# A row sum on one core: 127 consecutive rows to a partition, the last 128 rows one to a partition, and two stores on two queues

## The chip, the cores and the metric

The kernel runs on one core of a Trainium2 chip. The time is the device time of one execution in microseconds (us).

A profile names engines: DVE is VectorE, ACT is ScalarE, SP is SyncE. "SPq" and "ACTq" are the sequencers of SP and ACT issuing DMAs. HBM is the chip's main memory, where the input and the output lie; a partition is one of the 128 rows of the on-chip memory. A DMA is a copy between the two: the DMA engines carry it out in packets, and each engine that takes part reports a completion. "Landing" is the moment at which a DMA's completion has fully arrived.

## The reference

```python
batch, seq, dim = 32, 512, 1024
x = np.random.randn(batch, seq, dim).astype(np.float32)     # 67.1 MB
def reference(x, multiplier):                                # multiplier 0.5
    return (np.sum(x, axis=-1) * multiplier).astype(np.float32)
```

Seen flat, 16,384 rows of 4 KiB each become 16,384 floats (64 KiB).

## The kernel before

Each of the 128 partitions owns 128 consecutive rows. Seven blocks of 16 rows a partition (8.39 MB each) stream through three buffers; DVE reduces half of a block in one instruction, ACT the other half row by row. The eighth block comes in pieces of 8, 5 and 2 rows and one row cut in two, so that little work is left when the last byte arrives. Then one store writes everything.

```python
    rows = N // P                                            # 128
    x_rows = x_flat.rearrange("(p c) d -> p c d", p=P)       # partitions 512 KiB apart
    out_view = out.rearrange("b s -> (b s)").rearrange("(p c) -> p c", p=P)
    # ... seven blocks: nc.sync.dma_start(out=t, in_=x_rows[:, c0 : c0 + B, :])
    pieces = [(0, 8), (8, 13), (13, 15)]
    # ... the pieces, then the last row in two: in_=x_rows[:, c0 + B - 1, lo:hi]
    dve_span(t, B - 1, 0, cut, part)                         # first 640 columns of the last row
    dve_span(t, B - 1, cut, D, res[:, rows - 1 : rows], start=part)
    # ... a wait of the sync queue for the loads and ACT
    store = nc.sync.dma_start(out=out_view, in_=res)         # 128 runs of 512 bytes
```

Of the kernel before, what the change touches and what calls it, by code (L numbers as in the profile page):

```python
# [1 line left out]

# [4 lines left out]


@with_exitstack
def kernel(  # L10
    ctx: ExitStack,
    tc: tile.TileContext,
    x: bass.AP,
    multiplier: float,
    out: bass.AP,
):







    nc = tc.nc
    P = nc.NUM_PARTITIONS
    fp32 = mybir.dt.float32
    ADD = mybir.AluOpType.add

    x_flat = x.flatten_outer_dims()
    N, D = x_flat.shape  # L30
    rows = N // P
    x_rows = x_flat.rearrange("(p c) d -> p c d", p=P)
    out_view = out.rearrange("b s -> (b s)").rearrange("(p c) -> p c", p=P)
    mul = float(multiplier)

    B = 16
    n_blocks = rows // B
    assert N == P * rows and rows == n_blocks * B

    x_pool = ctx.enter_context(tc.tile_pool(name="x", bufs=3))  # L40
    res_pool = ctx.enter_context(tc.tile_pool(name="res", bufs=1))
    sums = res_pool.tile([P, rows], fp32, name="sums")
    res = res_pool.tile([P, rows], fp32, name="res")
    part = res_pool.tile([P, 1], fp32, name="part")

    loads = []
    acts = []

    def act_row(t, r, col):
        acts.append(nc.scalar.activation(  # L50
            out=t[:, r, :],
            in_=t[:, r, :],
            func=mybir.ActivationFunctionType.Copy,
            scale=mul,
            accum_out=res[:, col : col + 1],
        ))

    def dve_span(t, r, lo, hi, dst, start=0.0):
        mid = (lo + hi) // 2
        nc.vector.tensor_tensor_reduce(  # L60
            out=t[:, r, lo:mid],
            in0=t[:, r, lo:mid],
            in1=t[:, r, mid:hi],
            scale=mul,
            scalar=start,
            op0=ADD,
            op1=ADD,
            accum_out=dst,
        )

    for b in range(n_blocks - 1):
        c0 = b * B
        t = x_pool.tile([P, B, D], fp32, name="xb")
        loads.append(nc.sync.dma_start(out=t, in_=x_rows[:, c0 : c0 + B, :]))  # L74
        h = B // 2
        nc.vector.reduce_sum(  # L76
            out=sums[:, c0 : c0 + h], in_=t[:, 0:h, :], axis=mybir.AxisListType.X
        )
        nc.vector.tensor_single_scalar(  # L79
            out=res[:, c0 : c0 + h],  # L80
            in_=sums[:, c0 : c0 + h],
            scalar=mul,
            op=mybir.AluOpType.mult,
        )
        for r in range(h, B):
            act_row(t, r, c0 + r)

    c0 = (n_blocks - 1) * B
    t = x_pool.tile([P, B, D], fp32, name="xb")
    cut = 640  # L90
    pieces = [(0, 8), (8, 13), (13, 15)]
    for lo, hi in pieces:
        loads.append(
            nc.sync.dma_start(  # L94
                out=t[:, lo:hi, :], in_=x_rows[:, c0 + lo : c0 + hi, :]
            )
        )
    for lo, hi in ((0, cut), (cut, D)):
        loads.append(
            nc.sync.dma_start(  # L100
                out=t[:, B - 1, lo:hi], in_=x_rows[:, c0 + B - 1, lo:hi]
            )
        )
    on_act = {4, 5, 6, 7, 11, 12, 14}
    for r in range(B - 1):
        if r in on_act:
            act_row(t, r, c0 + r)
        else:
            dve_span(t, r, 0, D, res[:, c0 + r : c0 + r + 1])
    dve_span(t, B - 1, 0, cut, part)  # L110
    dve_span(t, B - 1, cut, D, res[:, rows - 1 : rows], start=part)



    seen = nc.sync.nop()
    for i in loads[-8:] + acts[-1:]:
        tc.add_manual_dep(
            seen.ins,
            i.ins.name,
            mybir.DependencyInfo(mybir.DependencyClass.Sync, mybir.DependencyReason.DATA),  # L120
            reason="ends seen early",
        )
    store = nc.sync.dma_start(out=out_view, in_=res)
    tc.add_manual_dep(
        store.ins,
        seen.ins.name,
        mybir.DependencyInfo(mybir.DependencyClass.NoSync, mybir.DependencyReason.SCHED_ONLY),
        reason="in this order",
    )

    def start_loads_at_entry(nc_):



        entry, *rest = nc_.main_func.blocks
        is_sp = lambda i: i.engine == mybir.EngineType.SP
        is_load = lambda i: type(i).__name__ == "InstDMACopy"
        for block in rest:
            body = list(block.instructions)
            own = [i for i in body if is_sp(i)]  # L140
            if not any(is_load(i) for i in own):
                continue
            lead = []
            for i in own:
                if not is_load(i) or i.sync_info.on_wait:
                    break
                lead.append(i)
            names = {i.name for i in lead}
            block.instructions = [i for i in body if i.name not in names]
            head = list(entry.instructions)  # L150
            at = next(
                k for k, i in enumerate(head) if is_sp(i) and type(i).__name__ == "InstDrain"
            )
            entry.instructions = head[:at] + lead + head[at:]
            return

    nc.at_finalize(start_loads_at_entry)


# [1 line left out]
_INS = ['x', 'multiplier']  # L161
_OUTS = [((32, 512), 'float32')]

_NUMBERS = {'multiplier': 0.5}


# [26 lines left out]
```

## Time and profile before

162.84 us (median of 3 runs, 162.84 to 163.09). Lines of the profile page:

```profile
span 161.1 us, 233 instructions
DVE 68.1 (42%) x34; ACT 67.9 (42%) x127; POOL 0.2 (0%) x4
...
DMA 86%; DVE 11%; SPq 1%; issue 0%; DVEq 0%
...
out_dram<-res SPq DMA_DIRECT2D x1, 64.0 KB, 1.6
```

The first line with percentages gives the busy time of each engine; the next is the chain of waits that ended last, as shares of the span; the last is the store: one issue, 64 KB, 1.6 us from issue to landing. DMA rules the chain, and the compute engines are idle more than half of the time.

The view of the block reduction (operation, count, duration, first and last start in us):

```profile
L76 DVE TENSOR_REDUCE sums<-xb x7: 8686/8686/8686, 22.4 to 138.6; 128x8 f32<-128x8192 f32 x7
```

Six steps from 22.4 to 138.6 us are 19.4 us each, for 8.39 MB: 433 GB/s. In the packet records, the median 64 KiB packet occupies its DMA engine for 2.418 us; 16 engines at that pace are 433.6 GB/s. The Trainium skill, "DMA: Bandwidth & Descriptors", section "Where 436 GB/s comes from", gives 435.2 GB/s as the ceiling of the ports; the trace agrees to 0.4%.

The end of the timeline (start, duration, engine):

```profile
157.68 0.49 DVE L60 CUSTOM_DVE_ANT_0 xb<-xb 128x320 f32<-128x320 f32 x1
...
158.26 0.42 DVE L60 CUSTOM_DVE_ANT_0 xb<-xb,part 128x192 f32<-128x192 f32 x1
158.60 0.08 DVE L60 DVE_READ_ACCUMULATOR2_ANT res<- 128x1 f32 x1
158.78 0.35 SPq L123 DMA_DIRECT2D out_dram<-res  x1
```

So the tail is: two short reductions, the store at 158.78, 1.6 us until it lands, and some 0.7 us of closing work. Nothing hides the landing of the last store.

### The profile page before, as it was taken

Reading aid. Unit: us, or ns where it says so; the run is one execution under the profiler, and the core shown is the slowest. Engines: PE = TensorE matmul, PEld = TensorE weight load, DVE = VectorE, ACT = ScalarE, POOL = GpSimd, SP = SyncE. Lnnn points to the kernel's source line nnn. Section 1 sums busy time; section 2 is a strip of 40 time slices with the busy share of each in tenths; the row PEclk is TensorE's granted clock in tenths of the full one; section 3 lists DMA queues with packets and bytes.
Section 4 is the critical chain, followed back from the end, with each engine's and each line's share of the span. In section 5 each row is a group of like instructions: output and inputs, shape, how many; then the busy total and the mean of one; then the engine's idle time right before and its main releaser. Section 6 shows DMA issues by size and latency. Waiting matters only on the chain.

```text
span 161.1 us, 233 instructions
## 1 busy us (share of the span) xinstructions
DVE 68.1 (42%) x34; ACT 67.9 (42%) x127; POOL 0.2 (0%) x4
## 2 busy tenths in 40 slices
DVE  0000049700695008930099102990049700697453
ACT  3000049600694008920099001980039700596862
POOL 0000000000000000000000000000000000000000
DMA  7997997997997997997997998998998998999990
GB/s 260 521 456 325 521 456 325 521 456 325 521 456 325 521 456 325 521 439 342 521 439 344 521 423 358 521 423 358 521 407 374 521 407 374 415 439 411 423 381 30
DMA packets 1873, 67.18 MB, mean 417 GB/s; under 512 B 208, under 2 KB 464, under 8 KB 592
## 3 DMA queue, kind: packets, MB, share of 16 engines
q1 hardware_dynamic: 1872, 67.18, 96.9%
q14 instruction: 1, 0.01, 0.0%
HBM read 67.11 MB, written 0.07 MB: 417 GB/s over the span
## 4 chain that ended last, share of the span: by engine, by line
DMA 86%; DVE 11%; SPq 1%; issue 0%; DVEq 0%
DMA xb<-in_x_dram 86%; DVE sums L76 11%; SPq L94 1%; DVE xb L60 1%; SPq L74 0%; DVE part L60 0%; DVEq L188 0%
## 5 line engine op out<-in xcount | busy, mean ns | idle before, releaser
L50 ACT ACTIVATE xb<-xb 128x1024 f32<-128x1024 f32 x63 | 65.6, 1043 | 88.4 <-DMA xb<-in_x_dram 88.4
L76 DVE TENSOR_REDUCE sums<-xb 128x8 f32<-128x8192 f32 x7 | 60.8, 8686 | 85.2 <-DMA xb<-in_x_dram 85.2
L50 ACT ACTIVATION_READ_ACCUMULATOR xb<-xb 128x1 f32 x63 | 11.8, 187 | 0.0
L60 DVE CUSTOM_DVE_ANT_0 xb<-xb 128x512 f32<-128x512 f32 (+1 forms) x9 | 5.6, 667 | 5.1 <-DMA xb<-in_x_dram 4.9
L50 ACT ACT_TABLE_LOAD x1 | 1.3, 1283 | 1.7 <-PEq L174 1.7
L79 DVE TENSOR_SCALAR res<-sums 128x8 f32<-128x8 f32 x7 | 1.2, 172 | 0.2
L60 DVE DVE_READ_ACCUMULATOR2_ANT res<- 128x1 f32 x9 | 0.7, 82 | 0.0
L60 DVE CUSTOM_DVE_ANT_0 xb<-xb,part 128x192 f32<-128x192 f32 x1 | 0.4, 418 | 0.1
L174 POOL MEMSET const-bfloat16-1.0<- 128x1 bf16 x1 | 0.1, 101 | 0.0
L174 POOL MEMSET const-uint8-127<- 128x1 uint8 x1 | 0.1, 101 | 0.0
L174 POOL MEMSET const-float32-0.0<- 128x1 f32 x1 | 0.1, 98 | 0.2 <-issue 0.2
L174 POOL MEMSET const-float32-1.0<- 128x1 f32 x1 | 0.1, 98 | 0.0
L60 DVE DVE_READ_ACCUMULATOR2_ANT part<- 128x1 f32 x1 | 0.1, 81 | 0.0
## 6 DMA issues: line engine op xcount, KB each, us to landing
xb<-in_x_dram SPq DMA_DIRECT2D x1, 4096.0 KB, 39.6
xb<-in_x_dram SPq DMA_DIRECT2D x1, 2560.0 KB, 45.4
xb<-in_x_dram SPq DMA_DIRECT2D x1, 1024.0 KB, 47.4
xb<-in_x_dram SPq DMA_DIRECT2D x1, 320.0 KB, 47.7
xb<-in_x_dram SPq DMA_DIRECT2D x1, 192.0 KB, 47.6
xb<-in_x_dram SPq DMA_DIRECT2D x7, 49.3
out_dram<-res SPq DMA_DIRECT2D x1, 64.0 KB, 1.6
```

The lines of the kernel that those rows point to most:

```text
L50: acts.append(nc.scalar.activation(out=t[:, r, :], in_=t[:, r, :], func=mybir.ActivationFunctionType.Copy, scale=mul, accum_out=res[:, col ...
L60: nc.vector.tensor_tensor_reduce(out=t[:, r, lo:mid], in0=t[:, r, lo:mid], in1=t[:, r, mid:hi], scale=mul, scalar=start, op0=ADD, op1=ADD, ...
L76: nc.vector.reduce_sum(out=sums[:, c0 : c0 + h], in_=t[:, 0:h, :], axis=mybir.AxisListType.X)
L79: nc.vector.tensor_single_scalar(out=res[:, c0 : c0 + h], in_=sums[:, c0 : c0 + h], scalar=mul, op=mybir.AluOpType.mult,)
L94: nc.sync.dma_start(out=t[:, lo:hi, :], in_=x_rows[:, c0 + lo : c0 + hi, :])
L174: nc = _bacc.Bacc("TRN2", target_bir_lowering=False, num_devices=1)
```

## The change

Its intent: move the partitions off a power-of-two distance in HBM (508 instead of 512 KiB), send most of the result out before the last reduction is done, and leave only 512 bytes for the end.

```diff
-    x_rows = x_flat.rearrange("(p c) d -> p c d", p=P)
-    out_view = out.rearrange("b s -> (b s)").rearrange("(p c) -> p c", p=P)
+    own = rows - 1
+    x_rows = x_flat[0 : P * own, :].rearrange("(p c) d -> p c d", p=P)
+    x_last = x_flat[P * own : N, :]
+    out_flat = out.rearrange("b s -> (b s)")
+    out_rows = out_flat[0 : P * own].rearrange("(p c) -> p c", p=P)
+    out_last = out_flat[P * own : N].rearrange("(p c) -> p c", p=P)
...
-    res = res_pool.tile([P, rows], fp32, name="res")
+    res = res_pool.tile([P, own], fp32, name="res")
+    last = res_pool.tile([P, 1], fp32, name="last")
...
-                out=t[:, B - 1, lo:hi], in_=x_rows[:, c0 + B - 1, lo:hi]
+                out=t[:, B - 1, lo:hi], in_=x_last[:, lo:hi]
...
-    dve_span(t, B - 1, cut, D, res[:, rows - 1 : rows], start=part)
+    dve_span(t, B - 1, cut, D, last, start=part)
+    nc.scalar.dma_start(out=out_rows, in_=res)
...
-    for i in loads[-8:] + acts[-1:]:
+    for i in loads[-8:]:
...
-    store = nc.sync.dma_start(out=out_view, in_=res)
+    store = nc.sync.dma_start(out=out_last, in_=last)
```

The result of the last 128 rows is one float in each of 128 partitions, and these floats are neighbours in memory: the last store is 128 writes of 4 bytes, packed into 512 bytes.

## The prediction

> **What bounds the kernel now.** The load stream. In the chain of waits DMA holds 86% of the 161.1 us span; DVE and ACT are busy 42% each and spend 85 and 88 us waiting for loads (waits view). The instructions of the reduce line start every 19.4 us (22.4 to 138.6 us, six steps): 8.39 MB per 19.37 us is 433 GB/s. The packet records of the trace agree: a 64 KiB packet takes 2.418 us on its engine, at median, in every 10 us stretch; 16 engines give 433.6 GB/s. The sync queue waits 86 us for buffers but always has an earlier load still running, so the stream does not pause. The Trainium skill ("DMA: Bandwidth & Descriptors", "Where 436 GB/s comes from") puts the port ceiling at 435 GB/s; the trace is within 0.5% of it.
>
> **What the change is after.** Two things. (1) Rows of neighbouring partitions lie 512 KiB apart; the same page ("Latency and other measured facts") reports 207 GB/s per direction at that pitch and 214 when padded by 4 KiB. This trace shows no such 3% loss: reading runs at full rate. What pitch could still cost is small: all 896 big packets together took 12.1 us more than at 2.418 us each, 0.76 us per engine. Of that, 0.53 us per engine is in the first packet of each engine (2.5 to 3.2 us), when all engines start at once on addresses that are multiples of 512 KiB apart. With 508 KiB they start apart. I expect about half of it back: -0.3 us. It may instead be a cold start, then nothing.
> (2) The store. Now: last piece lands 157.65, two half-row reduces 0.49 + 0.42 us, store issued 158.78 (0.35 us on the sync queue), landing 1.6 us after issue, then the end. After: 65 KB go from the ACT queue when row 13 (DVE) and ACT's last row, about 158.0 us, are done; they land near 159.7 (estimate: the same issue-to-landing of 1.6 us), before the last store's landing. Left last are 128 elements of 4 bytes: 8 packets per engine. Packets of 512 bytes took 27 ns, those of 4 bytes 9 ns, so about 0.14 us (8 x 18 ns) less. The rest of the 1.6 us is latency and stays. Against it: one more completion to wait for at the end, and many 4-byte writes into the same 512 bytes. Net -0.1 us, give or take 0.3.
>
> Nothing else moves: same bytes, same 64 KiB runs, same reduces; the last row's loads read one contiguous block, in packets of 2560 and 1536 bytes as before.
>
> **Predicted**: 162.84 - 0.3 - 0.1 = about 162.5 us, 161.9 to 163.2. Faster by over 2%: 0.02; within 2%: 0.95; slower: 0.03.
>
> **What would show it.** Reduce starts stay 19.37 us apart and the 64 KiB packets at 2.418 us (port-bound, pitch irrelevant to the rate). The first reduce starts at 22.0 to 22.4 instead of 22.4: if it moves, the first packets shrank. The final store is still issued near 158.4 to 158.8 and lands 1.3 to 1.7 us later; the ACT store lands earlier and is not in the chain.
>
> **What would make it wrong.** A gain over 2% (3.3 us) would need the packets to run faster than 2.418 us, so that figure would not be a ceiling. A loss would come from the 4-byte writes being slow when 16 engines write the same few lines of memory, from the 508-byte runs delaying the final store, or from 508 KiB being worse for the memory than 512, seen as big packets above 2.418 us.

## The result

168.34 us (median of 5 runs, 168.26 to 168.72) against 162.93 (5 runs, 162.84 to 163.21): ratio 1.0336, 95% interval 1.032 to 1.0351, so clearly slower. Here and below, a ratio and its interval come from the runs of both kernels and are not quite the ratio of the medians quoted.

The page after, the same lines as before:

```profile
span 166.5 us, 236 instructions
DVE 68.1 (41%) x34; ACT 67.9 (41%) x127; POOL 0.2 (0%) x4
...
DMA 83%; DVE 11%; SPq 1%; issue 0%; DVEq 0%
...
out_dram<-res ACTq DMA_DIRECT2D x1, 63.5 KB, 1.7
out_dram<-last SPq DMA_DIRECT2D x1, 0.5 KB, 7.1
```

The block reduction, and the end of the timeline:

```profile
L82 DVE TENSOR_REDUCE sums<-xb x7: 8685/8686/8687, 22.2 to 138.4; 128x8 f32<-128x8192 f32 x7
```

```profile
157.55 0.49 DVE L66 CUSTOM_DVE_ANT_0 xb<-xb 128x320 f32<-128x320 f32 x1
...
157.92 0.37 ACTq L118 DMA_DIRECT2D out_dram<-res  x1
...
158.13 0.42 DVE L66 CUSTOM_DVE_ANT_0 xb<-xb,part 128x192 f32<-128x192 f32 x1
158.47 0.08 DVE L66 DVE_READ_ACCUMULATOR2_ANT last<- 128x1 f32 x1
158.58 0.35 SPq L130 DMA_DIRECT2D out_dram<-last  x1
```

Until the last store's issue everything is as good as before or 0.2 us better: the reductions are still 19.4 us apart, and the store starts at 158.58 instead of 158.78. Then 512 bytes need 7.1 us to land where 64 KB needed 1.6. That is 5.5 us more, less the 0.2 us: 5.3 of the 5.4 us by which the span grew (166.5 - 161.1).

The chain of waits ends with the last engine instruction and does not show this wait. It stands in the waits of the sync queue, where the program ends (first the kernel before, then after; total, times, longest):

```profile
SPq L188 <- DMA out_dram<-res: 1.2, 1, 1.2
```

```profile
SPq L195 <- DMA out_dram<-last: 6.0, 1, 6.0
SPq L195 <- DMA out_dram<-res: 0.7, 1, 0.7
```

Where in the DMA is the time? The view of DMA traffic of the kernel after, for 158.5 to 166.5 us in 40 slices of 0.2 us, says: not in moving bytes.

```profile
GB/s 0 104 219 3 1 1 0 0 0 0 0 0 0 0 0 0 0 0 0 0 0 0 0 0 0 0 0 0 0 0 0 0 0 0 0 0 0 0 0 0
```

From the seventh slice (159.7 us) on, nothing is moved. The packet and completion records, read out of the traces:

| kernel | last store issued | its packets are done | first and last of 16 completions |
|---|---|---|---|
| before, 128 runs of 512 bytes | 158.78 | 159.98 | 160.15, 160.33 |
| after, 128 packed writes of 4 bytes | 158.58 | 159.63 | 161.63, 165.69 |

By their packet records, the DMA engines are done with the last 4-byte write 1.1 us after the issue; before, it was 1.2 us. What is late is the confirmation: in the kernel before, the completions come 0.2 to 0.4 us after the last packet is done, in the changed one 2.0 to 6.1 us after. The Trainium skill, "DMA: Bandwidth & Descriptors", section "Anatomy of one DMA — SWDGE (gpsimd) path", calls this part the write receipt of the target memory and says, of DMAs issued by GpSimd, that most of the fixed cost is spent there. The stores here come from the sync queue: the changed kernel's agrees about the place (6.1 of its 7.1 us), the store before does not (0.4 of its 1.6 us).

### The profile page after: what moved, and what is told of

Read it like the earlier page. It is cut to its first block, busy times and chain, and to the rows that moved or that the text cites. A ratio compares the mean times of both kernels' runs of the same rounds, so it can differ in the third digit from the quotient of the medians.

```text
span 166.5 us, 236 instructions
## 1 busy us (share of the span) xinstructions
DVE 68.1 (41%) x34; ACT 67.9 (41%) x127; POOL 0.2 (0%) x4
## 4 chain that ended last, share of the span: by engine, by line
DMA 83%; DVE 11%; SPq 1%; issue 0%; DVEq 0%
DMA xb<-in_x_dram 83%; DVE sums L82 10%; SPq L100 1%; DVE xb L66 1%; SPq L80 0%; DVE part L66 0%; DVEq L195 0%
```

## The experiments

Four theories. **A**: many small writes into the same short stretch of memory are taken one after another. **B**: each 4-byte write is slow wherever it goes. **C**: the two stores, or the two queues, collide. **D**: the new distance of the partitions, or the place of the last rows, costs time.

### The new distance alone

The changed loads, but one store of 512 bytes a partition. The output is in the wrong order.

```diff
-    res = res_pool.tile([P, own], fp32, name="res")
-    last = res_pool.tile([P, 1], fp32, name="last")
+    res = res_pool.tile([P, rows], fp32, name="res")
...
-    nc.scalar.dma_start(out=out_rows, in_=res)
...
-    store = nc.sync.dma_start(out=out_last, in_=last)
+    store = nc.sync.dma_start(out=out_flat.rearrange("(p c) -> p c", p=P), in_=res)
```

> Loads as in the changed kernel (508 KiB pitch, last 128 rows one to a partition), but one store of 512 bytes a partition on the sync queue, as before; the output is in the wrong order on purpose. Theory A (many 4-byte writes into the same lines of memory are taken one after another), B (each 4-byte write is slow, wherever it goes) and C (the two stores on two queues collide): the store lands in 1.6 us again and the time is 162.5 to 162.9 us, 0.0 to 0.3 under the kernel before. Theory D (the pitch or the last rows' place costs time at the end): stays near 168.

162.76 us (5 runs) against 163.02 (9 runs): ratio 0.999, interval 0.9975 to 1.0004. The store lands as before:

```profile
out_dram<-res SPq DMA_DIRECT2D x1, 64.0 KB, 1.6
```

D falls: the loads of the change cost nothing. Whether they gain 0.1% is not settled; the interval holds 1.

### The two stores alone

The loads as before, 127 columns from ACT and the last column from the sync queue. Its 128 writes of 4 bytes are now 512 bytes apart. The result is right.

```diff
+    last = res_pool.tile([P, 1], fp32, name="last")
...
-    dve_span(t, B - 1, cut, D, res[:, rows - 1 : rows], start=part)
+    dve_span(t, B - 1, cut, D, last, start=part)
+    nc.scalar.dma_start(out=out_view[:, 0 : rows - 1], in_=res)
...
-    store = nc.sync.dma_start(out=out_view, in_=res)
+    store = nc.sync.dma_start(out=out_view[:, rows - 1 : rows], in_=last)
```

> Loads as before (512 KiB pitch), but two stores on two queues: 127 columns from ACT, the last column from the sync queue as 128 writes of 4 bytes, now 512 bytes apart. The result is right. Theory A: the last store lands in 1.4 to 2 us, the time is within 0.5 us of the kernel before. Theory B: it lands in about 7 us again, time about 168.3. Theory C: about 7 us as well, since both queues and both stores are still there.

162.78 us against 163.02: ratio 0.9988, interval 0.9975 to 1.0. The DMA issues of its page:

```profile
out_dram<-res ACTq DMA_DIRECT2D x1, 63.5 KB, 1.6
out_dram<-last SPq DMA_DIRECT2D x1, 0.5 KB, 1.4
```

The same 128 writes of 4 bytes, from the same partitions, on the same two queues at about the same moment, land in 1.4 us when they are apart, and all completions come between 160.02 and 160.18 us. B and C fall with one run. What is left is the packing, or the place of these 512 bytes in the output, which the second repair below tests.

### The last store with nothing beside it

```diff
-    nc.scalar.dma_start(out=out_rows, in_=res)
```

> The changed kernel without the store of the 127 columns (wrong result on purpose), so that nothing is in flight when the 512 bytes are stored. Theories A and B: they still need about 7 us to land, time about 168. Theory C: 1.6 us to land, time about 162.6.

168.22 us (one run; the result is wrong).

```profile
out_dram<-last SPq DMA_DIRECT2D x1, 0.5 KB, 7.1
```

The other store has no part in it; C falls a second time.

### How it depends on distance, size and number

A probe without the reduction: 44 stores on the sync queue (22 different ones, twice), each issued after the one before has landed. The page on DMA that the expectation names is cited under "One engine or sixteen". Such lines make it up (`strided(n, w, step)` takes n runs of w floats, `step` floats apart):

```python
    put(lambda: nc.sync.dma_start(out=strided(128, 1, 1), in_=res[0:128, 0:1]))
    put(lambda: nc.sync.dma_start(out=strided(128, 1, 2), in_=res[0:128, 0:1]))
```

> A probe, no reduction (wrong result on purpose): 42 stores on the sync queue, each after the one before has landed: 4-byte writes from 128 partitions 4 to 512 bytes apart; runs of 8 to 512 bytes, packed; 64, 32, 16 partitions; 127 partitions, which the page on DMA says go to one engine; one run of 512 bytes. Theory A: 128 writes of 4 bytes land in about 7 us when packed and fall with the distance, to 1.6 us at 512 bytes, halving with each doubling of distance until one write has a line to itself; 64, 32 and 16 packed writes need about 4.3, 3.0 and 2.3 us; 127 packed writes from one engine need about the 7 us that 16 engines need, and little when apart. Theory B: about 7 us at every distance, about 1.6 + 5.5/2, /4, /8 us for 64, 32, 16 writes, and 127 writes on one engine need some 90 us (16 times 5.5), packed or apart.

In its timeline (start and duration of the issue), the difference of two starts is the landing of one store and about 0.1 us:

```profile
4.39 0.33 SPq L52 DMA_DIRECT2D out_dram<-res  x1
11.90 0.33 SPq L53 DMA_DIRECT2D out_dram<-res  x1
15.86 0.33 SPq L54 DMA_DIRECT2D out_dram<-res  x1
17.86 0.33 SPq L55 DMA_DIRECT2D out_dram<-res  x1
19.35 0.33 SPq L56 DMA_DIRECT2D out_dram<-res  x1
```

These are 4-byte writes at 4, 8, 16 and 32 bytes' distance: 7.51, 3.96, 2.00 and 1.49 us. Every case ran twice, the second time in reverse order:

| store | us from start to start, twice |
|---|---|
| 128 writes of 4 bytes, 4 bytes apart (packed) | 7.51, 8.61 |
| 8 bytes apart | 3.96, 3.32 |
| 16 bytes apart | 1.99, 1.45 |
| 32, 64, 128, 256, 512 bytes apart | 1.46 to 1.92 |
| 128 packed runs of 8 bytes | 3.11, 3.47 |
| 128 packed runs of 16 bytes | 2.40, 1.46 |
| 128 packed runs of 32 to 256 bytes | 1.46 to 1.52 |
| 64, 32, 16 packed writes of 4 bytes | 6.71 and 8.66; 4.72 and 5.30; 2.55 and 2.29 |
| 128 packed runs of 508 bytes; of 512 bytes | 1.73, 1.92; 1.62 (the second ended the probe) |
| 127 partitions, packed / 512 bytes apart | 10.52 and 8.76 / 2.65 and 2.64 |
| one run of 512 bytes from one partition | 1.12, 1.12 |

The direction is A's, its numbers only in part. The cost falls faster than I had said: 16 bytes' distance is already nearly free. And 64 packed writes cost as much as 128, where I had expected half of the excess. B is far off: 127 writes apart take 2.65 us, not 90.

### One engine or sixteen

The Trainium skill, "DMA: Bandwidth & Descriptors", section "Why a DMA increments its semaphore by 16 and not by 1", says that the number of DMA engines of such a copy is the largest up to 16 that divides its slowest dimension: 1 for 127 partitions, 2 for 122, 4 for 124. The completion records agree: besides the immediate update at about 0.4 us, one arrives for 127, two for 122 and four for 124. So a second probe of the same form can vary the engines, three passes:

> A probe like the one before (wrong result on purpose), three passes: 127 four-byte writes from one DMA engine at 4, 8, 16, 32, 64, 128 and 512 bytes' distance; then packed 4-byte writes from 31, 17 (one engine each), 122, 124, 128, 48, 96 and 112 partitions (2, 4, 16, 16, 16, 16 engines by the page's rule). If the writes into one 64-byte stretch are taken one after another whoever sends them, 127 packed writes need 7 to 10 us with 1, 2, 4 or 16 engines, and the excess over 512-byte distance falls with distance: about half at 8 bytes, under 1 us from 32 bytes on; 31 and 17 writes on one engine about 1/4 and 1/8 of the excess of 127. If instead it is engines getting in each other's way, fewer engines need less: 2 engines well under 7 us.

```profile
2.68 0.31 SPq L51 DMA_DIRECT2D out_dram<-res  x1
11.41 0.23 SPq L52 DMA_DIRECT2D out_dram<-res  x1
```

The distance of the two starts (8.72 us before rounding) is the first figure of the table, 127 packed writes on one engine:

| store of 4-byte writes | engines | us from start to start, three times |
|---|---|---|
| 127, packed | 1 | 8.72, 8.78, 9.46 |
| 127, 8 bytes apart | 1 | 4.78, 4.46, 5.17 |
| 127, 16 to 512 bytes apart | 1 | 2.65 to 2.68 |
| 122, packed | 2 | 9.85, 8.38, 9.64 |
| 124, packed | 4 | 7.33, 6.80, 6.46 |
| 128, packed | 16 | 7.73, 8.24, 9.71 |
| 48, 96 packed | 16 | 7.07, 6.64, 5.51; 7.07, 6.68, 7.17 |
| 112 packed | 16 | 7.37, 5.77 (the third ended the probe) |
| 31, 17 packed | 1 | 3.27, 4.63, 3.47; 2.48, 2.89, 2.49 |

Between 1 and 16 engines, 122 to 128 packed writes keep within 6.5 to 9.9 us here. So it is not engines disturbing each other. Sixteen of them don't share the work either, which suggests a limit in a place that they have in common; that is argued, not shown. The packet records point the same way: with 127 writes on one engine, the last packet is done 1.54 to 1.57 us after the issue at every distance, packed too, but the completion comes at 2.6 us from 16 bytes on and at 8.6 to 9.4 us when packed. At 8 bytes' distance the excess over writes apart is 1.8 to 2.5 us, about a third of the packed one, where half was expected. On one engine, 126 further writes cost 2.65 - 1.12 = 1.53 us when apart (an estimate of 12 ns each, from the two rows of the tables), and (8.72 - 1.12)/126 = 60 ns or more each when packed (an estimate too). The smaller cases were mis-sized in the expectation: by that 12 ns a write, 31 and 17 writes apart would need about 1.5 and 1.3 us, so they carry 1.8 to 3.1 and 1.2 to 1.6 us of excess, more than the 1/4 and 1/8 of the 6.1 to 6.8 us of 127 that I had expected. How the excess grows with the number of writes stays open.

### The dose in the kernel itself: runs of 8, 16 and 32 bytes

The changed kernel, with the last 256, 512 or 1024 rows going 2, 4 or 8 to a partition. The last store then has packed runs of 8, 16 or 32 bytes. All results are right. The first of them, cut (left out: a helper that picks the column of the result, the last row's new index, and the wait of the sync queue for ACT's last row):

```diff
-    own = rows - 1
+    G = 2
+    own = rows - G
...
-    last = res_pool.tile([P, 1], fp32, name="last")
+    last = res_pool.tile([P, G], fp32, name="last")
...
-    pieces = [(0, 8), (8, 13), (13, 15)]
+    pieces = [(0, 8), (8, 14)]
...
+    for lo, hi in [(14, 15)]:
+        loads.append(
+            nc.sync.dma_start(out=t[:, lo:hi, :], in_=x_last[:, lo - f : hi - f, :])
+        )
```

> The changed kernel with the last 256 rows two to a partition, so that the last store has packed runs of 8 bytes instead of 4; correct. From the probe (3.1 and 3.5 us from one store to the next against 7.5 and 8.6 for 4 bytes and 1.6 for 512): theory A expects 2.7 to 3.5 us to land and a time of about 164.0 to 165.0. If the change's loss came from anything but the size of the packed writes: 7 us and 168.

> The same with four rows to a partition, packed runs of 16 bytes; correct. The probe had 2.4 and 1.5 us, so theory A expects 1.4 to 2.4 us to land and 162.5 to 163.6.

> The same with eight rows to a partition, packed runs of 32 bytes; correct. Theory A: 1.4 us to land, 162.4 to 162.8.

The DMA issues of the last store, with 2, 4 and 8 rows, one kernel each:

```profile
out_dram<-last SPq DMA_DIRECT2D x1, 1.0 KB, 3.1
```

```profile
out_dram<-last SPq DMA_DIRECT2D x1, 2.0 KB, 1.4
```

```profile
out_dram<-last SPq DMA_DIRECT2D x1, 4.0 KB, 1.4
```

| bytes a run | landing us | time us (4 runs; before: 163.19) | ratio, interval |
|---|---|---|---|
| 8 | 3.1 | 165.01 | 1.011, 1.0095 to 1.0125 |
| 16 | 1.4 | 163.15 | 1.0001, 0.998 to 1.0022 |
| 32 | 1.4 | 162.84 | 0.9981, 0.9966 to 0.9996 |

This is the probe's curve inside the kernel: 7.1, 3.1, 1.4, 1.4 us. With more bytes to store, the store is faster. The 8-byte case lost 1.8 us, somewhat more than its 1.5 us of landing: in its timeline the store is issued only at 159.39 us, after a wait of 0.7 us for ACT. All three landings are in their expected ranges; the times of the first and the third lie 0.01 and 0.04 us above theirs.

### Two repairs

The first gives 112 rows to a partition (448 KiB apart) and the last 2048 rows 16 to a partition; the last store has runs of 64 bytes. The core of the edit:

```diff
-    own = rows - 1
+    own = rows - 16
...
+    x_last = x_last.rearrange("(p c) d -> p c d", p=P)
...
-    last = res_pool.tile([P, 1], fp32, name="last")
+    last = res_pool.tile([P, 16], fp32, name="last")
...
-                out=t[:, lo:hi, :], in_=x_rows[:, c0 + lo : c0 + hi, :]
+                out=t[:, lo:hi, :], in_=x_last[:, lo:hi, :]
```

> A repair, correct: partitions own 112 rows (448 KiB apart) and the last 2048 rows go 16 to a partition, so that the last store has runs of 64 bytes, which landed as fast as 512-byte runs in the probe. Theory A (what costs is many small writes into one 64-byte stretch): lands in about 1.4 us, time 162.3 to 162.8, so about 5.7 us under the changed kernel. If packed runs of 64 bytes cost too beside the other store: 164 or more.

162.72 us (5 runs) against 162.9 (9 runs): ratio 0.9984, interval 0.9972 to 0.9997; the result is right.

```profile
out_dram<-res ACTq DMA_DIRECT2D x1, 56.0 KB, 8.3
out_dram<-last SPq DMA_DIRECT2D x1, 8.0 KB, 1.4
```

The 8.3 us of the first line are harmless: here the store from ACT was issued at 147.28 us, among the loads, and its last completion came at 155.58 us, 3 us before the last store was issued.

The second keeps the change as it is, but turns the 128 sums on DVE into 4 partitions of 32 and stores 4 runs of 128 bytes into the same 512 bytes:

```diff
-    last = res_pool.tile([P, 1], fp32, name="last")
+    last = res_pool.tile([P, 32], fp32, name="last")
+    turned = res_pool.tile([P, 32], fp32, name="turned")
+    nc.gpsimd.memset(last, 0.0)
...
+    nc.vector.transpose(turned, last)
...
-    store = nc.sync.dma_start(out=out_last, in_=last)
+    store = nc.sync.dma_start(out=out_flat[P * own : N].rearrange("(g c) -> g c", g=4), in_=turned[0:P:32, :])
```

> A repair, correct: the changed kernel, but the last 128 sums are turned on DVE into 4 partitions of 32, and the last store has 4 runs of 128 bytes into the same 512 bytes. Theory A: lands in 1.0 to 1.3 us; the turn costs 0.1 to 0.3 us on DVE; time 162.2 to 162.8. If the cost lay in the place (the last 512 bytes of the output) or in the late second queue and not in the number of small writes: 7 us to land and about 168.

163.17 us against 162.9: ratio 1.0014, interval 1.0 to 1.0028; right. The loss of the change is gone, though the bytes go to the same place at the same late moment. It gains nothing over the kernel before, by its timeline: the turn takes 0.21 us, and the issue of this store 0.64 us instead of 0.35. The time missed its expected range by 0.4 us, and the landing missed its own: the page gives none, but the last completion record is at 160.52 us, 1.6 us after the issue began, where 1.0 to 1.3 us were expected. The wait at the end of the program is 0.8 us instead of 6.0:

```profile
SPq L198 <- DMA out_dram<-turned: 0.8, 1, 0.8
```

The turn and the issue in the timeline:

```profile
158.66 0.21 DVE L120 STREAM_TRANSPOSE turned<-last 128x32 f32<-128x32 f32 x1
158.90 0.64 SPq L133 DMA_DIRECT2D out_dram<-turned  x1
```

Two versions (32- and 64-byte runs) are 0.2% under the kernel before with an interval that leaves out 1. By the measure of 2% they count as the same: the stream is at its ceiling and the tail is short, so there was little to win.

## Why the prediction was wrong

- "Reduce starts stay 19.37 us apart": right, 19.35 us in most steps. The kernel is bound by the stream, and the distance of 508 KiB changed nothing in it.
- "I expect about half of it back: -0.3 us": the store did start 0.2 us earlier, but not for the reason given. The first packets did not shrink; their mean excess over 2.418 us grew from 0.52 to 0.75 us per engine, and it was 0.70 at 512 KiB in the run with the two stores alone. What differed was when they started, on average at 1.62 us before and 1.20 after. At 512 KiB two profiles have the first reduction at 22.26 and 22.40 us, at 508 KiB four have it at 22.03 to 22.32. A gain by distance is not settled.
- "The ACT store lands earlier and is not in the chain": right; it was issued at 157.92 and was complete at 159.63, against the 159.7 foretold.
- **The step that failed**: "Packets of 512 bytes took 27 ns, those of 4 bytes 9 ns, so about 0.14 us (8 x 18 ns) less. The rest of the 1.6 us is latency and stays." The last store landed in 7.1 us instead of 1.3 to 1.7. The first half of the step held: the store's own 4-byte packets took 9 ns (median), and its last packet was done 1.05 us after the issue instead of 1.20, so some 0.15 us less. Here was some luck: the 4-byte packets of the trace of before were most likely the completions and no stores, since 13 DMAs with 16 completions each make 208 of the 209 there were. What failed is "The rest of the 1.6 us is latency and stays". The rest, from the last packet to the last completion, was 0.35 us before (159.98 to 160.33) and 6.06 us after (159.63 to 165.69). A packet's time on its engine is not the time until the write is confirmed.
- The danger was named ("the 4-byte writes being slow when 16 engines write the same few lines of memory") but priced at 0.3 us, without a number for it in any trace. Its wording was half right: packing is what costs, but one engine alone pays as much as sixteen.

Shown: the loss is the landing of the last store; it comes from packed writes of 4 bytes, and not from their size alone, the number of engines, the second queue, the other store, the loads or the place in the output. Only argued: that the memory takes writes to one stretch in turn. That one engine and sixteen need the same time speaks for a place common to all engines; which one, and why 48 packed writes cost nearly as much as 128, is open.

## What to carry to other kernels

Don't end a kernel with a store of one element from each of 128 partitions into neighbouring addresses: here 512 bytes packed from 4-byte writes landed in 7.1 us, while 128 runs of 16 to 512 bytes, or 4-byte writes 512 bytes apart, landed in 1.4 to 1.6 (runs of 16 bytes once needed 2.4 in the probe). Price the last store by its time from issue to landing for the same pattern of addresses, not by bytes or by packet times, and leave each partition at least 16, better 32, adjacent bytes. When a stream is at its ceiling, a change of layout has almost nothing to win and can still lose in the tail.

## What the Trainium skill lacked or had wrong

- "DMA: Bandwidth & Descriptors", section "Specifications": the page names 512 bytes as the least transfer for full rate, with read-modify-write below it. For the landing of a small store the size was not what mattered: 128 writes of 4 bytes landed in 1.4 us at 512 bytes' distance and in 7.1 us when packed. No page has the cost of packed writes: 7.1 us for 4-byte runs, 3.1 for 8-byte runs, 1.4 from 16 bytes on.
- The same page, "Latency and other measured facts", reports 207 GB/s at a row distance of 512 KiB, and 214 at 4 MiB padded by 4 KiB, for copies between HBM tensors. For loads into SBUF alone this kernel shows no loss: 433 GB/s at 512 and at 508 KiB (19.35 us a block after the first in both).
- The same page, "Anatomy of one DMA — SWDGE (gpsimd) path", gives a nearly constant fixed cost of about 2 us for DMAs issued by GpSimd. For the stores from the sync queue here it is not constant: the same 512 bytes landed in 1.4 to 7.1 us, by the addresses alone.
